# One value projection of 512 columns, a new place for the convolution, and another order of the first operations, in a two-block transformer kernel

## The chip, the core and the metric

The kernel runs as one program on one core of a Trainium2 chip. The time is device time in microseconds (us) of an execution, the median of several runs. Engines: PE is TensorE (its weight loads are listed as PEld), DVE is VectorE, ACT is ScalarE, POOL is GpSimd, SP is SyncE, whose queue issues all DMAs here. Each engine works through its own instructions in a fixed order; waits go over semaphores.

## What is computed

Two blocks of two layers each, on 512 tokens of width 1024, in f32. The change touches the first block. One layer of it, cut from the reference:

```python
x = x + 0.5 * swiglu(rmsnorm(x, ffn1_norm), ffn1_gate, ffn1_up, ffn1_down)
z = rmsnorm(x, mix_norm) @ w_in
(aq, ak, av, iq, ik, iw, bq, bk, bv, bg, br, cu, dcq, dckv, dkpe) = jnp.split(z, ...)
y_a = dsa_mixer(aq, ak, av, iq, ik, iw, ...)   # attention over 128 selected keys (top-k of an index score)
y_b = gla_mixer(bq, bk, bv, bg, br, ...)       # gated linear attention
y_c = conv_mixer(cu, ...)                      # depthwise convolution, 31 taps, 256 channels
y_d = mla_mixer(dcq, dckv, dkpe, ...)          # attention over latents
x = x + jnp.concatenate([y_a, y_b, y_c, y_d], axis=-1) @ w_out
x = x + 0.5 * swiglu(rmsnorm(x, ffn2_norm), ffn2_gate, ffn2_up, ffn2_down)
```

The second block has other mixers and the same kind of FFN; nothing of it is edited, though it uses the old `values`.

## The kernel before

The activations lie transposed, eight tiles `x[k]` of 128 channels by 512 tokens. A product in f32 is made of three in a rounded format (fp32r): a tile is split into a high part h and a residual l, and `mm3` adds h.h, h.l and l.h (lines 205, 206, 207 of `mm3`; PE instructions of these lines are told apart by the tile that they write). Weights come in one fixed list (`plan`, made of each stage's `order`). `fill` takes the next one from the list: a DMA of 128 x 1024 f32 (512 KB) into one of three `raw` buffers (line 188), the high part `wh` on ACT (line 190), the residual `wl` on DVE (line 191), each in one of four buffers (NW2). `weights(src)` keeps three of them filled and hands out the first.

A planner arranges the instructions of each engine before the run: of those that it takes to be ready at a moment it issues the one that stands first in the program; what is ready it reckons from modelled durations, DMAs included. The order on each engine is fixed after that, so an instruction that was put early and whose data comes late holds up all behind it on its engine.

**The beginning.** `begin` issues the first weight load, the x tiles and the second weight load, then for each k the head `xn[k]` h on ACT (`norm_head`, line 296), the residual on DVE (`norm_rest`, line 300), and the squares: ACT makes the square (`norm_square`, line 310, two buffers `sq`), POOL adds it to `sqacc` (line 311). PE later takes the mean `ms` (line 318) from `sqacc`. `dense_first` makes the first two weights' products: for each k both outputs' products with xn[k] h (lines 224 and 225), then those with the residuals (line 262). Outputs are scaled by the reciprocal root only when they are read from PSUM, so the products do not need `ms`. FFN outputs have six PSUM buffers.

**The mixers of the first block** (`Mixers.run`). In order: `a_keys`, `d_latents`, `a_queries`, `a_index`, `d_heads` (with four `uv` projections of 256 columns, line 1073 evicts them), `c_prep` (the projections `cu2`, `cu0`, `cu3`, `cu1`; the gated channels go to DRAM as `hp_d`). Then the D attention runs in eight steps, each with one round of the top-k on DVE and three steps of a side chain: `c_conv`, `a_values`, `a_heads` (projections aq0, aq1, ak0, ak1), `c_out`. After it: `b_heads` (bq, bk), `b_values`, `b_gates` (br0, br1), `a_bias` (loads `toep`), and then the A attention with the B mixer as its side chain.

`c_conv` loads each half of the channels from `hp_d` in shifted copies into the one buffer `gq` (four DMAs, line 995), then runs 32 matmuls on it (line 1000, each listed as two instructions); it yields after the loads and after the matmuls of each half, so conv1's load can start only when conv0's matmuls have read the buffer. `values` (line 590 on) has the activations as the stationary operand and two weights of 4 x 256 columns as the moving one: four token tiles x 8 k x 3 products of 256 columns, called once for A (`av`) and once for B (`bv`).

Of the kernel before, what the change touches and what calls it, by code (L numbers as in the profile page):

```python
# [9 lines left out]
F32 = mybir.dt.float32  # L10
# [10 lines left out]
KD = D // 128  # L21
# [11 lines left out]
def pack_values(w):  # L33

    return np.ascontiguousarray(w.reshape(2, 4, 128, 256).transpose(0, 2, 1, 3))

# [25 lines left out]
class Model:  # L62
# [115 lines left out]

    def fill(self, n):
# [62 lines left out]
    def dense_first(self, srcs, name, parts):  # L242
# [50 lines left out]
    def norm_head(self, k, gain, c=slice(0, S)):  # L293
        if c.start == 0:
            self.xn[k] = self.xn_tile(f"xn{k}h"), self.xn_tile(f"xn{k}l")
        self.nc.scalar.activation(self.xn[k][0][:, c], self.x[k][:, c], AF.Copy, scale=self.vec(gain, 1, k))

    def norm_rest(self, k, gain, c=slice(0, S)):
        h, l = self.xn[k]
        self.nc.vector.scalar_tensor_tensor(l[:, c], self.x[k][:, c], self.vec(gain, 1, k), h[:, c].bitcast(F32),  # L300
                                            op0=ALU.mult, op1=ALU.subtract)

    def norm_square(self, k, eng=None):
        nc = self.nc
        if self.sq_acc is None:
            self.sq_acc = self.tmp.tile([128, S], F32, name="sqacc", tag="sqacc", bufs=1)
            nc.scalar.activation(self.sq_acc, self.x[k], AF.Square)
            return
        sq = self.sq()
        nc.scalar.activation(sq, self.x[k], AF.Square)  # L310
        (eng or nc.gpsimd).tensor_tensor(self.sq_acc, self.sq_acc, sq, op=ALU.add)  # L311
# [71 lines left out]
NRAW = 3  # L383
NW2 = 4
# [98 lines left out]
def host_pack_mixers(I, P, vadd):  # L483
    for l in range(2):
# [9 lines left out]
        P[f"w_v{l}"] = np.stack([pack_values(w[:, IN_OFF[n]:IN_OFF[n] + 256]) for n in ("av", "bv")])  # L494
# [109 lines left out]


# [65 lines left out]
class Mixers(Phase):  # L671


    def order(self):
# [3 lines left out]
        v = lambda i: [ap[f"w_v{l}"][i, c] for c in range(2)]  # L678
        return p("misc", "dcq0", "dcq1", "dckv", "iq0", "iq1") + [ap[f"d_uq{l}"], ap[f"d_ukv{l}"]] + \
            p("cu2", "cu0", "cu3", "cu1") + v(0) + p("aq0", "aq1", "ak0", "ak1", "bq", "bk") + v(1) + p("br0", "br1") + \  # L680
# [137 lines left out]
    def b_values(self):  # L818
        two = [self.z(f"vB{i}", f"R{i}") for i in range(2)]
        self.vB = [two[t // 2][:, 256 * (t % 2):256 * (t % 2) + 256] for t in range(4)]  # L820
        self.values(self.ap[f"w_v{self.l}"][1], lambda t: self.vB[t])

    def a_values(self):
        two = [self.z(f"vA{i}", f"R{2 + i}") for i in range(2)]
        self.vA = [two[t // 2][:, 256 * (t % 2):256 * (t % 2) + 256] for t in range(4)]
        self.values(self.ap[f"w_v{self.l}"][0], lambda t: self.vA[t])
# [213 lines left out]
    def d_heads(self):  # L1040
# [25 lines left out]
        for t in range(4):  # L1066
            o = M.psum_mm("uv")[:, :256]
            r = slice(t * 128, (t + 1) * 128)
            M.mm3(o, (ch[:, r], cl[:, r]), (ukv[0][:, 256:512], ukv[1][:, 256:512]), True, True)
            if t % 2 == 0:  # L1070
# [915 lines left out]
```

## Time and profile before

| | us |
|---|---|
| median of 3 runs | 3255.04 (3254.06 to 3256.03) |
| the profiled execution | 3250.12 |
| its span, first to last instruction | 3248.3 |
| PE busy | 3179.6 |
| DVE busy | 1719.9 |
| ACT busy | 1314.0 |
| POOL busy | 151.6 |

Matmuls are pipelined, and a matmul's listed duration holds the time that it takes to pass through the array; so the distance from one start to the next tells what a matmul costs in a row of them. The granted TensorE clock of the whole execution is 0.997 of full speed; in the first microseconds the clock column says 1.00 also where the distances are those of half speed.

### The profile page before, as it was taken

The numbers are of one execution on the slowest core, as the hardware profiler recorded it, in microseconds if no ns is written. First come the engines' busy times: TensorE is split into PE (matmuls) and PEld (weight loads), VectorE is DVE, ScalarE is ACT, GpSimd is POOL, SyncE is SP. The second block draws the span as 40 slices with busy tenths as digits, with TensorE's granted clock in tenths as the row PEclk, the third lists the DMA queues.
The fourth block names the chain that finished last, engine by engine and source line by source line (L and its number), as shares of the span: only waits on it lengthen the run. The fifth ranks groups of instructions, "written<-read, shape, count | busy, mean of one in ns | idle before, by whom it ended". The sixth has DMA issues, their size and how long they took to land.

```text
span 3248.3 us, 39097 instructions
## 1 busy us (share of the span) xinstructions
PE 3179.6 (98%) x15294; PEld 2560.3 (79%) x15298; DVE 1719.9 (53%) x2788; ACT 1314.0 (40%) x2040; POOL 151.6 (5%) x153
## 2 busy tenths in 40 slices
PE   8999999999999999999999999999999999999998
PEld 6888866778888888875768888877888888788887
DVE  5443378664433444347775443588654427764432
ACT  4232345743322333244664332345643226753322
POOL 1000100010001000010000000100100010000000
PEclk9999999999999999999999999999999999999999
DMA  4333341133333333352113333322233332323332
GB/s 158 120 93 95 113 133 54 33 106 96 98 96 99 98 97 94 95 140 93 56 40 107 98 95 96 112 86 63 91 105 97 94 101 72 104 90 98 93 94 73
DMA packets 114473, 306.66 MB, mean 94 GB/s; under 512 B 21840, under 2 KB 35056, under 8 KB 114288
## 3 DMA queue, kind: packets, MB, share of 16 engines
q1 hardware_dynamic: 114288, 304.16, 31.2%
q8 instruction: 120, 1.97, 0.3%
q14 instruction: 65, 0.53, 0.0%
HBM read 292.18 MB, written 10.09 MB: 93 GB/s over the span
## 4 chain that ended last, share of the span: by engine, by line
PE 88%; ACT 4%; DVE 4%; DMA 2%; issue 1%; SPq 0%; POOL 0%; DVEq 0%; ACTq 0%
PE gu L206 14%; PE gu L205 14%; PE gu L207 14%; PE o L206 8%; PE o L205 8%; PE o L207 8%; DMA conv<-hp_d 2%; PE conv L1000 1%; PE wo L206 1%; PE wo L205 1%; PE wo L207 1%; PE v L207 1%; PE v L206 1%; PE v L205 1%; ACT gAqb L886 0%
## 5 line engine op out<-in xcount | busy, mean ns | idle before, releaser
L190 ACT ACTIVATE wh<-raw 128x1024 fp32r<-128x1024 f32 (+2 forms) x550 | 550.2, 1002 | 1479.3 <-PE gu L206 823.7
L191 DVE TENSOR_TENSOR wl<-raw,wh 128x1024 fp32r<-128x1024 f32 (+2 forms) x550 | 631.6, 1150 | 519.4 <-ACT wh L190 516.6
L205 PE MATMUL o<-hid,wh 128*128 128x512 f32 (+1 forms) x1100 | 419.2, 381 | 0.0
L206 PE MATMUL o<-hid,wh 128*128 128x512 f32 (+1 forms) x1100 | 418.9, 381 | 0.0
L207 PE MATMUL o<-hid,wl 128*128 128x512 f32 (+1 forms) x1100 | 418.5, 380 | 0.0
L351 DVE SCALAR_TENSOR_TENSOR us<-gu,rstd 128x512 f32<-128x512 f32 x130 | 89.9, 691 | 402.1 <-PE gu L207 401.7
L207 PEld LDWEIGHTS o<-hid,wl 128*128 128x128 f32 x1100 | 206.8, 188 | 39.8
L205 PEld LDWEIGHTS o<-hid,wh 128*128 128x128 f32 x1100 | 206.8, 188 | 39.6
L206 PEld LDWEIGHTS o<-hid,wh 128*128 128x128 f32 x1100 | 206.8, 188 | 39.3
L349 DVE SCALAR_TENSOR_TENSOR gs<-gu,rstd 128x512 f32<-128x512 f32 x130 | 89.9, 692 | 256.0 <-PE gu L207 255.3
L311 POOL TENSOR_TENSOR sqacc<-sqacc,sq 128x512 f32<-128x512 f32 x49 | 82.8, 1690 | 1580.6 <-ACT sq L310 1540.6
L354 ACT ACTIVATE hid<-gs 128x512 fp32r<-128x512 f32 x132 | 83.7, 634 | 94.8 <-DVE gs L352 94.8
L205 PE MATMUL gu<-xn0h,wh 128*128 128x512 f32 x254 | 101.3, 399 | 0.0
L206 PE MATMUL gu<-xn6l,wh 128*128 128x512 f32 x254 | 99.0, 390 | 1.9 <-DVE xn6l L300 1.9
L352 DVE TENSOR_TENSOR gs<-gs,us 128x512 f32<-128x512 f32 x132 | 91.3, 692 | 15.7 <-ACT gs L350 3.8
L206 PE MATMUL gu<-xn0l,wh 128*128 128x512 f32 x254 | 98.9, 389 | 0.0
L207 PE MATMUL gu<-xn1h,wl 128*128 128x512 f32 x254 | 98.9, 389 | 0.0
L205 PE MATMUL gu<-xn1h,wh 128*128 128x512 f32 x254 | 98.8, 389 | 0.0
L207 PE MATMUL gu<-xn0h,wl 128*128 128x512 f32 x254 | 98.8, 389 | 0.0
L206 PE MATMUL gu<-xn1l,wh 128*128 128x512 f32 x254 | 98.8, 389 | 0.0
L206 PE MATMUL gu<-xn2l,wh 128*128 128x512 f32 x254 | 98.8, 389 | 0.0
L205 PE MATMUL gu<-xn7h,wh 128*128 128x512 f32 x254 | 98.8, 389 | 0.0
(1438 smaller groups left out, 7079.1 us busy)
## 6 DMA issues: line engine op xcount, KB each, us to landing
raw<-in_ffn_gu SPq DMA_DIRECT2D x176, 512.0 KB
raw<-in_f_gu SPq DMA_DIRECT2D x88, 512.0 KB
raw<-in_ffn_d SPq DMA_DIRECT2D x64, 448.0 KB
raw<-in_w_in SPq DMA_DIRECT2D x36, 512.0 KB
raw<-in_ffn_d SPq DMA_DIRECT2D x32, 512.0 KB
raw<-in_f_d SPq DMA_DIRECT2D x32, 448.0 KB
raw<-in_w_out SPq DMA_DIRECT2D x32, 256.0 KB
raw<-in_f_d SPq DMA_DIRECT2D x16, 512.0 KB
```

The source lines that it names most:

```text
L190: nc.scalar.activation(h, raw, AF.Copy)
L191: nc.vector.tensor_tensor(l, raw, h.bitcast(F32), op=ALU.subtract)
L205: t.matmul(out, lhsT=wh, rhs=xh, start=first, stop=False)
L206: t.matmul(out, lhsT=wh, rhs=xl, start=False, stop=False)
L207: t.matmul(out, lhsT=wl, rhs=xh, start=False, stop=last)
L311: (eng or nc.gpsimd).tensor_tensor(self.sq_acc, self.sq_acc, sq, op=ALU.add)
L349: nc.vector.scalar_tensor_tensor(gs, g, -1.0, self.nrstd, op0=ALU.mult, op1=ALU.mult)
L351: nc.vector.scalar_tensor_tensor(us, u, -1.0, self.nrstd, op0=ALU.mult, op1=ALU.mult)
L352: nc.vector.tensor_tensor(gs, gs, us, op=ALU.mult)
L354: nc.scalar.activation(h, gs, AF.Copy)
L1000: nc.tensor.matmul(p[32 * g:32 * g + 32], lhsT=cw[:, g, k], rhs=st[:, g, 4 * k:4 * k + S], start=(k == 0), stop=(k == 7))
```

## The change

- `pack_wide` and `values_wide`: the A and B value weights are packed side by side, as four weights of 2 x 512 columns. One call, `ab_values`, makes both: four token tiles x 8 k x 3 products of 512 columns, one eviction per token tile, and it yields after each token tile. All four weights are held until the last token tile.
- The list of weights has the four value weights ahead of aq0; `b_values` after the D attention is gone.
- The side chain becomes: conv0's loads, the values, conv0's matmuls, conv1's loads, `a_heads`, conv1's matmuls, `c_out`.
- `d_heads`: the four `uv` projections go by twos into one PSUM tile, with one eviction of 512 columns each.
- `begin`: x tiles and halves (512 columns) of the first two weights are loaded in turn; the halves are split by ACT and DVE as they come. The order of ACT (heads and half copies, then squares) and of DVE (half residuals, xn residuals, then the additions of the squares, which leave POOL) is fixed by added dependencies without waits. 12 products of the constant `ones` tile with itself (128 x 128) go to a PSUM tile that nothing reads.
- `dense_first` for this beginning takes the first four k of the first output, then of the second, then the other four k of both.

```diff
+    def fill_part(self, i, part):
+        nc = self.nc
+        if part == 0:
+            src = self.todo.popleft()
...
+        c = slice(part * 512, part * 512 + 512)
+        nc.sync.dma_start(raw[:, c], flat[:, c])
+        if part == 1:
+            self.loaded.append((src, (h, l)))
+        return (lambda: nc.scalar.activation(h[:, c], raw[:, c], AF.Copy),
+                lambda: nc.vector.tensor_tensor(l[:, c], raw[:, c], h[:, c].bitcast(F32), op=ALU.subtract))
...
         for c in parts:
-            if c.start or not n:
+            if len(parts) == 1:
+                for o, w in zip(outs, ws):
+                    self.heads_first([o], [w], c, range(0, 4))
+                self.heads_first(outs, ws, c, range(4, KD))
+            elif c.start or not n:
                 self.heads_first(outs, ws, c)
...
+    def values_wide(self, w, out):
+        M, nc = self.M, self.nc
+        ws = [M.weights(w[c]) for c in range(4)]
+        for t in range(4):
+            r = slice(t * 128, (t + 1) * 128)
+            o = M.psum_mm("v")
+            for k in range(KD):
+                s = slice((k % 2) * 512, (k % 2) * 512 + 512)
+                M.mm3(o, (M.xn[k][0][:, r], M.xn[k][1][:, r]), (ws[k // 2][0][:, s], ws[k // 2][1][:, s]), k == 0, k == KD - 1)
+            nc.scalar.activation(out(t), o, AF.Copy, scale=self.rn[:, t:t + 1])
+            yield
...
-            p("cu2", "cu0", "cu3", "cu1") + v(0) + p("aq0", "aq1", "ak0", "ak1", "bq", "bk") + v(1) + p("br0", "br1") + \
+            p("cu2", "cu0", "cu3", "cu1") + v + p("aq0", "aq1", "ak0", "ak1", "bq", "bk", "br0", "br1") + \
...
-        for t in range(4):
-            o = M.psum_mm("uv")[:, :256]
...
+        for i in range(2):
+            o = M.psum_mm("uv")
+            dv = self.z(f"dv{i}", f"dv{i}")
+            for t in range(2):
...
+            nc.scalar.activation(dv, o, AF.Copy)
...
-            side = chain(self.c_conv, self.a_values, self.a_heads, self.c_out)
+            conv = self.c_conv()
+            part = lambda: next(conv)
+            side = chain(part, self.ab_values, part, part, self.a_heads, part, self.c_out)
...
-            self.b_values()
...
         def begin():
             M.norm_begin()
+            M.halved, split = [], []
             for k in range(KD):
-                if k in (0, 2):
-                    M.fill(1 + k // 2)
                 M.load_x(k)
+                if k < 4:
+                    split.append(M.fill_part(k // 2, k % 2))
+            head = lambda k: M.norm_head(k, "ffn1_norm0")
+            act, vec = [], []
             for k in range(KD):
-                M.norm_head(k, "ffn1_norm0")
-                M.norm_rest(k, "ffn1_norm0")
-            for k in range(KD):
-                M.norm_square(k)
+                act.append(head(k))
+                if k < 4:
+                    h, l = split[k]
+                    act.append(h())
+                    vec.append(l())
+            vec += [M.norm_rest(k, "ffn1_norm0") for k in range(KD)]
+            both = [M.norm_square(k, nc.vector) for k in range(KD)]
+            M.in_order(act + [a for a, _ in both])
+            M.in_order(vec + [v for _, v in both[1:]])
+            warm = M.psum("warm")
+            for i in range(WARM):
+                nc.tensor.matmul(warm[:, :128], lhsT=M.sumsq_ones, rhs=M.sumsq_ones, start=True, stop=True)
```

`in_order(ops)` adds such a dependency from each operation of the list to the next; `WARM` is 12.

## Rows read from the trace of the kernel before

**Rows 1.** The page, busy time and share of the span of each engine
```profile
PE 3179.6 (98%) x15294; PEld 2560.3 (79%) x15298; DVE 1719.9 (53%) x2788; ACT 1314.0 (40%) x2040; POOL 151.6 (5%) x153
```
**Rows 2.** The page, chain of work that ended last, share by engine
```profile
PE 88%; ACT 4%; DVE 4%; DMA 2%; issue 1%; SPq 0%; POOL 0%; DVEq 0%; ACTq 0%
```
**Rows 3.** PE's waits: in total, times, the longest
```profile
PE conv L1000 <- DMA conv<-hp_d: 12.5, 8, 2.8
...
PE uv L205 <- ACT uk L1060: 0.7, 2, 0.3
```
**Rows 4.** PE in order of time, beginning: start, duration, operation [idle before <-releaser]
```profile
7.19 0.80 PE L224 MATMUL gu<-xn0h,wh 128*128 128x512 f32 x1 [7.19 <-ACT xn0h L296]
...
11.73 0.63 PE L224 MATMUL gu<-xn1h,wh 128*128 128x512 f32 x1
...
14.66 0.39 PE L225 MATMUL gu<-xn3h,wl 128*128 128x512 f32 x1
...
22.51 1.13 PE L318 MATMUL ms<-sqacc,ones 128*128 128x512 f32 x2 [2.24 <-POOL sqacc L311]
...
28.05 0.39 PE L205 MATMUL gu<-xn0h,wh 128*128 128x512 f32 x1
...
33.27 0.39 PE L207 MATMUL gu<-xn7h,wl 128*128 128x512 f32 x1
```
**Rows 5.** ACT in order of time, beginning
```profile
20.00 0.71 ACT L296 ACTIVATE xn7h<-x,vecs 128x512 fp32r<-128x512 f32 x1
```
**Rows 6.** POOL in order of time, beginning
```profile
10.83 11.62 POOL L311 TENSOR_TENSOR sqacc<-sqacc,sq 128x512 f32<-128x512 f32 x7 [9.64 <-ACT sq L310]
```
**Rows 7.** Stretches: us, busy of PE, PEld, DVE, ACT, POOL, PEclk, DMA share, GB/s
```profile
0.00:5.00 5.00, 0.00 (x0) 0.00 (x0) 0.17 (x2) 1.28 (x1) 0.66 (x9) 1.00 0.59 176
5.00:10.00 5.00, 1.77 (x3) 0.86 (x3) 2.24 (x3) 3.63 (x5) 0.00 (x0) 1.00 1.03 378
```
**Rows 8.** DVE in order of time, an operation of two inputs and 512 columns
```profile
576.56 0.69 DVE L191 TENSOR_TENSOR wl<-raw,wh 128x512 fp32r<-128x512 f32 x1 [2.51 <-ACT wh L190]
```
**Rows 9.** PE in order of time, a 128x128 f32 product and its follower
```profile
479.89 0.38 PE L1118 MATMUL lgD<-dk,dq 128*128 128x128 f32 x2
480.11 0.22 PE L1119 MATMUL lgD<-causal_bf,ident_bf 128*128 128x128 bf16 x1
```
**Rows 10.** PE in order of time, first and last of 23 value products in a row
```profile
477.13 0.28 PE L205 MATMUL v<-wh,xn0h 128*128 128x256 f32 x1
...
479.77 0.29 PE L206 MATMUL v<-wl,xn7h 128*128 128x256 f32 x1
```
**Rows 11.** The chain in order of time, 440 to 580 us: start, us, what
```profile
450.03 13.32 DMA conv<-hp_d
```
**Rows 12.** PE in order of time, conv's matmuls in layer 0 and (last) layer 1
```profile
460.67 1.05 PE L1000 MATMUL conv<-conv 128*32 128x512 f32 x2 [0.27 <-DMA conv<-hp_d]
463.39 3.63 PE L1000 MATMUL conv<-conv 128*32 128x512 f32 x28 [1.67 <-DMA conv<-hp_d]
...
484.60 1.04 PE L1000 MATMUL conv<-conv 128*32 128x512 f32 x2 [1.09 <-DMA conv<-hp_d]
488.36 1.30 PE L1000 MATMUL conv<-conv 128*32 128x512 f32 x2 [2.72 <-DMA conv<-hp_d]
...
491.17 1.66 PE L1000 MATMUL conv<-conv 128*32 128x512 f32 x2
...
1516.86 1.92 PE L1000 MATMUL conv<-conv 128*32 128x512 f32 x2 [2.80 <-DMA conv<-hp_d]
```
**Rows 13.** PE in order of time, first product of B's values and of br
```profile
562.25 0.36 PE L205 MATMUL v<-wh,xn0h 128*128 128x256 f32 x1
...
577.13 0.40 PE L205 MATMUL br<-xn0h,wh 128*128 128x512 f32 x1
```
**Rows 14.** ACT and DVE in order of time, a weight's two parts after the cu projections
```profile
459.23 1.06 ACT L190 ACTIVATE wh<-raw 128x1024 fp32r<-128x1024 f32 x1 [0.91 <-PE cu L206]
...
468.15 1.22 DVE L191 TENSOR_TENSOR wl<-raw,wh 128x1024 fp32r<-128x1024 f32 x1
```

More of the change, by code (lines that the diff above doesn't have):

```diff
@@ L35, in pack_values, with pack_wide @@
     return np.ascontiguousarray(w.reshape(2, 4, 128, 256).transpose(0, 2, 1, 3))
+def pack_wide(w):
+    return np.ascontiguousarray(w.reshape(4, 2, 128, 512).transpose(0, 2, 1, 3))
 def cols(v):
@@ L177, in plan, with in_order @@
         self.todo, self.loaded = deque(srcs), deque()
+    def in_order(self, ops):
+        for a, b in zip(ops, ops[1:]):
+            self.tc.add_manual_dep(b.ins, a.ins.name, mybir.DependencyInfo(
+                mybir.DependencyClass.NoSync, mybir.DependencyReason.DATA), reason="issue order")
+    def fill_part(self, i, part):
+        nc = self.nc
+        if part == 0:
+            src = self.todo.popleft()
+            flat = src.rearrange("p a b -> p (a b)")
+            raw = self.wp.tile([128, flat.shape[1]], F32, name="raw", tag="raw", bufs=NRAW)
+            h, l = (self.wp.tile([128, flat.shape[1]], FR, name=n, tag=n, bufs=NW2) for n in ("wh", "wl"))
+            self.halved.append((src, flat, raw, h, l))
+        src, flat, raw, h, l = self.halved[i]
+        c = slice(part * 512, part * 512 + 512)
[4 more added lines that the diff above has]
+                lambda: nc.vector.tensor_tensor(l[:, c], raw[:, c], h[:, c].bitcast(F32), op=ALU.subtract))
     def fill(self, n):
@@ L295, in norm_head @@
             self.xn[k] = self.xn_tile(f"xn{k}h"), self.xn_tile(f"xn{k}l")
-        self.nc.scalar.activation(self.xn[k][0][:, c], self.x[k][:, c], AF.Copy, scale=self.vec(gain, 1, k))
+        return self.nc.scalar.activation(self.xn[k][0][:, c], self.x[k][:, c], AF.Copy, scale=self.vec(gain, 1, k))
     def norm_rest(self, k, gain, c=slice(0, S)):
         h, l = self.xn[k]
-        self.nc.vector.scalar_tensor_tensor(l[:, c], self.x[k][:, c], self.vec(gain, 1, k), h[:, c].bitcast(F32),
+        return self.nc.vector.scalar_tensor_tensor(l[:, c], self.x[k][:, c], self.vec(gain, 1, k), h[:, c].bitcast(F32),
                                             op0=ALU.mult, op1=ALU.subtract)
@@ L383 @@
 NRAW = 3
+WARM = 12
 NW2 = 4
@@ L493, in host_pack_mixers @@
         P[f"w_in{l}"] = pack_T(np.concatenate(t, axis=1))
-        P[f"w_v{l}"] = np.stack([pack_values(w[:, IN_OFF[n]:IN_OFF[n] + 256]) for n in ("av", "bv")])
+        P[f"w_v{l}"] = pack_wide(np.concatenate([w[:, IN_OFF[n]:IN_OFF[n] + 256] for n in ("av", "bv")], axis=1))
         uq = I["d_uq"][l].reshape(256, 4, 96)
@@ L815, in a_attend, with ab_values @@
                 yield
[L818 to L826, printed above, removed]
+    def ab_values(self):
+        v = [self.z(f"vAB{t}", f"R{t}") for t in range(4)]
+        self.vA = [t[:, :256] for t in v]
+        self.vB = [t[:, 256:] for t in v]
+        yield from self.values_wide(self.ap[f"w_v{self.l}"], lambda t: v[t])
     def b_heads(self):
```

20 lines of the change are left out of this document (8 added, 12 removed).

## The prediction

> **What bounds the kernel now.** I read the busy times first: TensorE (PE) is busy for 98% of the span, and no other engine comes near it [rows 1]. The chain that ended last says the same: 88% of it is PE work, and the next engine holds 4% [rows 2]. So a microsecond is worth something only where PE waits, where it runs at its lower clock level, or where it does work that can be had cheaper. The second thing to look at is therefore what PE waits for. The longest total is the conv matmuls of the first block's two mixers, which wait for their own DMAs; the small `uv` projections wait a little for ScalarE [rows 3]. Two places follow from that: the beginning, and the stretch from about 459 us (and the same 1028 us later in layer 1, 1516.86 against 488.36 us [rows 12]) in which conv, values and the D attention share PE.
>
> In the beginning the first matmul starts at 7.19 us, and the third FFN weight's products (L205) only at 28.05 us [rows 4]. The 48 products of the first two weights lie between. At the later spacing of 0.227 us (23 steps from 28.05 to 33.27 us) they would need 10.9 us. Two things stretch them. First, from 11.73 to 14.66 us the products stand 0.42 us apart (7 steps) and last 0.63 us, then 0.39 us: 512 columns in 0.42 us is the 1.2 GHz level, 0.227 us the 2.4 GHz level. The rise came after PE had worked without a gap since about 9.7 us. Second, the last activation tile's head, xn7h, is written by ScalarE only at 20.00 us [rows 5], since ScalarE makes the squares in the same order and each waits for a buffer that GpSimd frees: seven additions in 11.62 us [rows 6]. The mean of squares `ms` sits in PE's order ahead of xn7h and waits 2.24 us for the same additions [rows 4].
>
> The DMAs are not the limit there: 0.88 MB had come by 5 us (176 GB/s) and 1.89 MB more by 10 us [rows 7]. The eight x tiles, two weights and the vectors are 3.2 MB; at the latter rate, 378 GB/s, they are in by about 11.2 us.
>
> **The change, part by part.**
>
> *Beginning.* Added: two more DMA issues on SP (four half loads of 256 KB in place of two of 512 KB), each copied by ScalarE and subtracted by VectorE as 512 columns; removed: GpSimd's seven additions, which go to VectorE at 0.69 us each for two-input 512-column work [rows 8] against 1.66. ScalarE's order becomes heads and half copies, then squares; VectorE's becomes four half residuals, eight xn residuals, then additions. So xn7h no longer follows the squares: it follows its DMA. With about 1 us for landing and copy I put it at 12.3 us (estimate from rows 7), against 20.00. After it PE still owes 4 head products and 16 products on xn..l, 20 x 0.227 = 4.5 us, so 16.9 us at the least. The residuals are 12 x 0.69 = 8.3 us on VectorE, which starts at about 6 us and waits for halves on the way, so xnl7 comes at 14.5 to 16.3 us. PE also has a queue: o1's first products need the third and fourth half load, so some 24 head products remain at about 9 us, 5.5 us at the upper level; then 16 more, 3.6 us: 18 us. I take 18.5 us for the end of the first two weights, 17 if nothing queues, and 20 if the clock falls back in the sparse first microseconds. Against 28.05 that is 8 to 11 us.
>
> What is late next is the third weight: its residual is one VectorE operation which may stand behind the seven additions, 4.8 us after 16.3, so 21.1, and 1.2 us itself: 22.3. Then PE waits from 18.5 to 22 and the gain is 6. I take **-8 us**, ends -5 and -11. `ms` and the reciprocal root cannot cost more: six PSUM buffers let PE run 4 weights of 24 x 0.227 = 5.4 us ahead.
>
> The 12 constant products need only `ones`, written at 1 us. A 128x128 f32 product is listed as two instructions and the next one starts 0.22 us later [rows 9], at the upper level; 0.44 at the lower: 12 x 0.44 = 5.3 us, from 1.1 to 6.4 us. PE is otherwise idle until 7.19, so they cost at most a microsecond of the first products, which wait for later tiles anyway. What they may give, 15 products at 0.23 instead of 0.42 (2.9 us), is inside the 18.5; if the clock does not rise, the end is 20.
>
> *Values as 512 columns.* 192 products of 256 columns per layer become 96 of 512. The former stand 0.120 us apart (22 steps, 477.13 to 479.77 us) [rows 10], the latter 0.227 [rows 4]: 96 x (0.240 - 0.227) = 1.2 us, **-2.4 us** for two layers. The Trainium skill, "TensorE: Matmul & The Clock Gate", section "Back-to-back issue gap", speaks against this edit: it gives a spacing of columns by clock plus a fixed 2.5 ns, so two 256s would cost only 2.5 ns more than one 512, by that estimate 0.5 us in two layers and a sum smaller by 1.9 us. The trace disagrees with 12 ns a pair.
>
> *uv.* Four PSUM tiles and evictions become two. PE waits 0.7 us for them in two layers [rows 3]; the products are the same. I take **-0.7 us**, ends 0 and -0.7.
>
> *Values of B moved, conv order.* In the kernel before, conv's matmuls come in PE's order straight after the `cu` projection, because they precede the values in the program; their DMAs are not there. One conv load takes 13.32 us from issue to landing [rows 11]. So PE does two instructions from 460.67 to 463.39 us where a run of 28 takes 3.63 (0.13 each): 2.5 us lost. For conv1 it waits 1.09 and 2.72 us, and from 483.51 to 491.17 us it does two pairs and six value products (1.2 us): 6.5 us lost. Layer 1 shows the same wait, 2.80 us [rows 12]. That makes 9 us per layer. VectorE and ScalarE, which the D attention needs, stand still meanwhile, so neither is a bound that would take the gain over.
>
> After the change conv0's DMAs are issued, then all values come, then conv0's matmuls, conv1's DMAs, the A projections, conv1's matmuls. From 459 us PE has 96 x 0.227 = 21.8 us of value products to do, and only the last quarter of each tile needs the fourth weight; six of eight k, 18 products, are 4.1 us: to 463.1, as the conv data lands. I count the 2.5 us as won. conv1's load then runs beside three more value tiles (16.3 us) and the A projections; I count 4.5 of 6.5 us, since the order is still fixed at compile time without knowing the DMA's real length. B's values leave the stretch from 562.25 to 577.13 us, where PE works on them and then on `br` before the A attention can start [rows 13]; they fill the holes instead, which is how holes become time. Their two weights are no longer queued on SP behind the toep loads.
>
> New wait: four value weights fill all four wh/wl buffers. The fourth is copied after `cu` at 459.23 us, as another weight is now, and its residual can be late on VectorE; it was 468.15 us for the weight after the two values [rows 14], but there VectorE stood behind `sp`, which stood behind conv. I take 1 us. The next weight, aq0, can be copied only when the last value tile has passed the first weight, 18 products or 4.1 us before its own start; copy and residual take 1.06 + 1.22 us [rows 14], so it fits unless VectorE is inside a top-k round; 1 us. What is queued behind those two on ScalarE and VectorE are the D attention's exponentials and the top-k. Ends: 0 and 6 us per layer. **Net -2.5 - 4.5 + 2 = -5 per layer, -10 us**, ends -18 and +3 (nothing won but 1.5 us per layer of new wait).
>
> Sum: -8 - 2.4 - 0.7 - 10 = **-21 us**. The profiled execution took 3250.1 us for a span of 3248.3; it would take 3229. The median of the runs, 3255.0, is 4.9 us above that execution, so the predicted median is **3234 us**.
>
> **The rivals.** (1) *The conv wait stays*: the planner again puts conv where PE looks free, ahead of its data. [rows 3, 12] speak for it: eight waits, in both layers alike. Then 3255 - 8 - 2.4 - 0.7 + 0 = 3244. (2) *Slower: the value weights starve the next ones.* While four weights hold all wh/wl buffers none is prepared; if aq0's residual stands behind one whole step of the D attention (eight steps from 479.89 [rows 9] to at most 577.13 us [rows 13]: 12 us), PE stops for 12 us, and again for layer 1, while conv's waits stay: 3255 - 11 + 24 = 3268. It decides from a net loss of 5.5 us per layer on. Against it: the copy can start 4.1 us early, and `wl` operations in that stretch are placed between top-k rounds. (3) *The beginning gives little*: `wl` of the third weight and `ms` stand behind the additions and PE waits to 25: -3, mixers as forecast: 3239. (4) *The holes close wholly* (both conv loads hidden, no new wait): 3255 - 10 - 2.4 - 0.7 - 18 = 3224, and a little less where conv also runs in one piece.
>
> **How the numbers follow.** Forecast with (4), which is its lower side: 0.66; (1) 0.15; (3) 0.09; (2) 0.08; nothing to see 0.02. The time is the forecast's, 3234. Range: low -21 and the ends of its terms (-11 - 2.4 - 0.7 - 18 = -32, and 4 more for conv in one piece): 3219; high -5 - 2.4 + 0 + 0 = 3248, which takes in (1) and (3). A measurement of this kernel tells about 0.2%, 6.5 us, from no change. Faster by more: 0.66 + 0.09 + 0.10 of (1) = 0.85; within: 0.05 of (1) + 0.02 + 0.01 = 0.08; slower: 0.07.
>
> **What would show each step.** Right: xn7h by 13 us, L205 of the third weight between 17 and 22 us, products 0.23 us apart from about 7 us on; value products 0.227 us apart, 96 per layer; conv's wait for its DMA from 12.5 to below 5 us; `br` and the A attention 7 us earlier relative to the start of the mixer. Wrong: a new long wait of the third weight or of `aq` for wl, conv's matmuls again in pairs with gaps, or a D attention that ends later than before relative to the mixer's start.

## The result, and the profile after

| | us |
|---|---|
| before, median of the runs beside it | 3254.55 (3251.99 to 3256.03) |
| after, median of 4 runs | 3222.69 (3222.01 to 3224.93) |
| ratio, 95% interval | 0.991 (0.9898 to 0.9923) |
| profiled execution, before and after | 3250.12 and 3222.01 |
| its span, before and after | 3248.3 and 3220.2 |

The change takes about 32 us off the median and 28.1 off the span of the profiled execution. The page of after, busy time by engine and the shares of the chain that ended last, answers to [rows 1, 2]:

```profile
PE 3171.1 (98%) x15126; PEld 2551.9 (79%) x15130; DVE 1723.1 (54%) x2797; ACT 1306.3 (41%) x2026; POOL 138.6 (4%) x146
...
PE 91%; ACT 4%; DVE 4%; issue 1%; DMA 0%; SPq 0%; DVEq 0%; ACTq 0%
```

The 2% that DMA held in the chain are gone. Of the saving in the spans, 8.5 us are PE busy time and the rest is time in which PE had stood idle. In PE's waits of after (total, times, the longest) the line of conv and that of `uv` [rows 3] no longer stand. The longest, and one that is new, are

```profile
PE lev L934 <- ACT gAqb L928: 4.3, 8, 1.2
...
PE bd L898 <- DVE bpd L895: 2.9, 2, 1.4
```

The first total was there before (4.4 us); the second was not, and it marks where part of the gain is given back: `bd`, a small product of the B mixer, waits for DVE.

**The beginning of after.** PE in order of time (start, duration, operation, [idle before <-releaser]) answers to [rows 4]; the products with xn[k] h in `dense_first` are now lines 252 and 253, `mm3` is lines 233 to 235:

```profile
1.05 5.49 PE L1988 MATMUL warm<-ones 128*128 128x128 f32 x24 [1.05 <-DVE eps L86]
6.62 0.57 PE L252 MATMUL gu<-xn0h,wh 128*128 128x512 f32 x1
...
10.16 0.50 PE L252 MATMUL gu<-xn3h,wh 128*128 128x512 f32 x1 [0.78 <-ACT xn3h L328]
10.50 0.40 PE L253 MATMUL gu<-xn3h,wl 128*128 128x512 f32 x1
...
19.59 0.39 PE L233 MATMUL gu<-xn0h,wh 128*128 128x512 f32 x1
...
27.75 1.02 PE L349 MATMUL ms<-sqacc,ones 128*128 128x512 f32 x2
```

From 10.50 us on nothing is missing: 40 products of 0.227 us lead to the third weight at 19.59 us (28.05 before), and `ms` waits for nothing. ACT and then DVE in the same stretch:

```profile
12.71 0.72 ACT L328 ACTIVATE xn7h<-x,vecs 128x512 fp32r<-128x512 f32 x1
```
```profile
15.94 0.74 DVE L332 SCALAR_TENSOR_TENSOR xn7l<-x,vecs,xn7h 128x512 fp32r<-128x512 f32 x1
16.60 0.69 DVE L342 TENSOR_TENSOR sqacc<-sqacc,sq 128x512 f32<-128x512 f32 x1
17.20 1.22 DVE L219 TENSOR_TENSOR wl<-raw,wh 128x1024 fp32r<-128x1024 f32 x1
18.34 0.68 DVE L342 TENSOR_TENSOR sqacc<-sqacc,sq 128x512 f32<-128x512 f32 x1
```

The third weight's residual stands between two additions and not behind seven, so PE does not wait for it.

**The mixer of layer 0 in after**, PE in order of time, answers to [rows 10, 12, 13]:

```profile
450.88 0.39 PE L233 MATMUL v<-wh,xn0h 128*128 128x512 f32 x1
...
456.10 0.39 PE L235 MATMUL v<-wh,xn7l 128*128 128x512 f32 x1
...
465.05 2.76 PE L1042 MATMUL conv<-conv 128*32 128x512 f32 x18
...
554.44 0.40 PE L233 MATMUL br<-xn0h,wh 128*128 128x512 f32 x1
...
566.33 1.08 PE L879 MATMUL pre<-misc,bup 128*128 128x512 f32 x2
```

Value products stand 0.227 us apart (23 steps), conv waits for no DMA, and `br` starts 22.7 us earlier than in [rows 13]. But `pre`, the small product with which the B mixer's gates begin, now comes after `br`; before it came 17 us ahead of it:

```profile
559.94 1.02 PE L837 MATMUL pre<-misc,bup 128*128 128x512 f32 x2
```

The conv waits of before had a second price. The stretch around them in before (us, busy of PE, PEld, DVE, ACT, POOL, PEclk, DMA share, GB/s):

```profile
482.00:495.00 13.00, 9.20 (x41) 4.29 (x39) 5.19 (x21) 3.88 (x16) 0.00 (x0) 0.87 0.38 117
```

Behind conv's wait of 2.72 us the granted clock fell to the 1.2 GHz level for part of the stretch (0.13 x 13 = 1.7 us of clock): the value products from 489.97 to 490.82 us stand 0.21 us apart instead of 0.12. Layer 1 shows the same (0.86 from 1512 to 1524 us). In after PE is busy without a gap from 450 to 490 us, and the clock reads 1.00.

**Where the time went.** For one mixer I added, tile by tile, the distances from each PE row to the next start, so that a wait is charged to the tile before it. The rows are to be read to 0.2 us. Layer 0, from the mixer's first projection to the next FFN, in us (the kernels other than before and after are the experiments below; "A/B stage" is `wo`, `lgA` and `gB`):

| kernel | mixer | conv | values | uv | A/B stage | the rest |
|---|---|---|---|---|---|---|
| before | 306.35 | 25.26 | 26.57 | 2.40 | 77.77 | 174.35 |
| after | 295.97 | 16.26 | 23.34 | 1.67 | 81.43 | 173.27 |
| order_narrow | 293.22 | 15.28 | 24.00 | 2.39 | 78.10 | 173.45 |
| wide_old_order | 309.63 | 25.50 | 24.96 | 2.40 | 82.82 | 173.95 |
| narrow_moved | 297.22 | 15.24 | 23.84 | 2.40 | 81.42 | 174.32 |
| begin_order_narrow | 296.13 | 18.00 | 25.36 | 1.67 | 77.63 | 173.47 |
| early_prep | 292.49 | 16.25 | 23.32 | 1.67 | 78.06 | 173.19 |
| gates_late | 299.77 | 16.28 | 23.31 | 1.66 | 79.27 | 179.25 |

After against before: conv -9.0, values -3.2, uv -0.7, the rest -1.1, A/B stage +3.7, together -10.4. Layer 1 gives -11.4 in the same way (conv -10.1). With -7.6 at the beginning that is -29.4 at the end of the first block; 1.3 us are given back in the second block. About 0.8 of it goes behind a wait that both kernels have there, 2.57 us of PE for ACT (tile `glu`): in the stretch around it the clock is lower in after, and not in before. After, then before:

```profile
2218.00:2226.00 8.00, 5.33 (x33) 4.04 (x32) 6.74 (x14) 5.49 (x12) 0.00 (x0) 0.79 0.50 158
```
```profile
2247.40:2255.40 8.00, 5.21 (x36) 3.13 (x34) 7.13 (x16) 6.12 (x14) 0.00 (x0) 1.00 0.52 160
```

The rest goes around 2742 us, where PE waits 1.4 us for a weight's residual (tile `xb`) instead of 0.5.

The medians lie 3.8 us further apart than the spans. The profiled execution of before, 3250.12, lies below all four runs of its median, and one reason shows. In its beginning the clock stays at 1.00 behind the 2.24 us wait of `ms` (20 to 30 us), while order_narrow, narrow_moved and only_mix, which begin in the same way, read 0.83 there and wide_old_order 0.66; their mixers start at 382.1 to 383.2 us, that of before at 380.45. Against those four the new beginning is worth 9 to 10 us at that point, and 7.6 against the execution of before that was profiled.

### The profile page after: what moved, and what is told of

The parts are those of the page before. It is cut to its first block, busy times and chain, and to the rows that moved or that the text cites. A ratio compares the mean times of both kernels' runs of the same rounds, so it can differ in the third digit from the quotient of the medians.

```text
span 3220.2 us, 38750 instructions
## 1 busy us (share of the span) xinstructions
PE 3171.1 (98%) x15126; PEld 2551.9 (79%) x15130; DVE 1723.1 (54%) x2797; ACT 1306.3 (41%) x2026; POOL 138.6 (4%) x146
## 4 chain that ended last, share of the span: by engine, by line
PE 91%; ACT 4%; DVE 4%; issue 1%; DMA 0%; SPq 0%; DVEq 0%; ACTq 0%
PE gu L233 14%; PE gu L234 14%; PE gu L235 14%; PE o L234 8%; PE o L235 8%; PE o L233 8%; PE conv L1042 1%; ACT gAqb L928 1%; PE v L233 1%; PE v L234 1%; PE v L235 1%; PE wo L233 1%; PE wo L234 1%; PE wo L235 1%; PE lgD L1160 1%
## 5 line engine op out<-in xcount | busy, mean ns | idle before, releaser
L218 ACT ACTIVATE wh<-raw 128x1024 fp32r<-128x1024 f32 (+3 forms) x548 | 547.9, 1002 | 1481.0 <-PE gu L234 815.8
L219 DVE TENSOR_TENSOR wl<-raw,wh 128x1024 fp32r<-128x1024 f32 (+3 forms) x548 | 629.4, 1150 | 497.0 <-ACT wh L218 491.3
L342 POOL TENSOR_TENSOR sqacc<-sqacc,sq 128x512 f32<-128x512 f32 x42 | 69.9, 1665 | 1544.3 <-ACT sq L341 1504.8
L233 PE MATMUL gu<-xn4h,wh 128*128 128x512 f32 x254 | 99.2, 391 | 0.0
L235 PE MATMUL gu<-xn6h,wl 128*128 128x512 f32 x254 | 98.8, 389 | 0.0
```

The source lines that it names most:

```text
L218: nc.scalar.activation(h, raw, AF.Copy)
L219: nc.vector.tensor_tensor(l, raw, h.bitcast(F32), op=ALU.subtract)
L233: t.matmul(out, lhsT=wh, rhs=xh, start=first, stop=False)
L235: t.matmul(out, lhsT=wl, rhs=xh, start=False, stop=last)
```

## The experiments

Each was compared with runs of before on the same chip (the medians of before there lie within 0.4 us of each other; beside after it was 3254.55):

| kernel | median, us | before, us | ratio, 95% interval |
|---|---|---|---|
| only_begin | 3244.32 | 3252.46 | 0.9974 (0.9964 to 0.9984) |
| only_mix | 3231.85 | 3252.46 | 0.9936 (0.9921 to 0.9950) |
| order_narrow | 3226.05 | 3252.46 | 0.9917 (0.9902 to 0.9932) |
| wide_old_order | 3258.51 | 3252.46 | 1.0019 (1.0010 to 1.0029) |
| early_prep | 3215.38 | 3252.81 | 0.9887 (0.9872 to 0.9901) |
| gates_late | 3226.79 | 3252.81 | 0.9920 (0.9906 to 0.9935) |
| begin_order_narrow | 3222.18 | 3252.81 | 0.9906 (0.9889 to 0.9922) |
| narrow_moved | 3235.06 | 3252.81 | 0.9945 (0.9930 to 0.9959) |
| no_warm | 3225.41 | 3252.40 | 0.9918 (0.9904 to 0.9932) |
| begin_order | 3224.42 | 3252.40 | 0.9914 (0.9900 to 0.9927) |
| pool_adds | 3230.51 | 3252.40 | 0.9934 (0.9920 to 0.9947) |
| prep_four_uv | 3216.08 | 3252.40 | 0.9889 (0.9876 to 0.9903) |

### The two halves of the change: only_begin and only_mix

only_begin is after with the mixers of before; only_mix is after with the beginning of before. In terms of the change, only_begin leaves out

```diff
-            self.b_values()
...
-            side = chain(self.c_conv, self.a_values, self.a_heads, self.c_out)
+            side = chain(part, self.ab_values, part, part, self.a_heads, part, self.c_out)
```

with the `uv` pairs and the list of weights that belong to it, and only_mix leaves out

```diff
-                if k in (0, 2):
-                    M.fill(1 + k // 2)
...
+            both = [M.norm_square(k, nc.vector) for k in range(KD)]
+            M.in_order(act + [a for a, _ in both])
+            M.in_order(vec + [v for _, v in both[1:]])
...
+                nc.tensor.matmul(warm[:, :128], lhsT=M.sumsq_ones, rhs=M.sumsq_ones, start=True, stop=True)
```

with the halved loads and the new order of `dense_first`.

> The beginning of the changed kernel alone; values, uv and conv order as before. Theory (the parts add, since PE bounds every stage between): 7 to 9 us less than before, all of it there when the third weight's products start (19.6 instead of 28.05 us), and unchanged to the end. Rival (a later stage takes it back, as the second block seems to take 1.2 us): less than 5 us.

> The mixers' part alone (512-column values, uv by twos, conv order); beginning as before. Theory (the parts add): 20 to 24 us less than before, conv's wait for its DMA gone, 10 to 11.5 us in each layer. Rival (the mixers gain only with the other beginning, by a different plan): below 15 us.

Measured: -8.1 and -20.6 us, both as expected, together -28.7 against the -28.1 of the spans (the medians' -31.9 lies 3 us further off). The parts add up as far as that spread allows. By the tiles that PE writes, its order in the mixers is that of before in only_begin and that of after in only_mix (but for two records of some 1500 that one trace of each pair lacks): the new beginning doesn't change it.

### The order alone, the wide form alone: order_narrow and wide_old_order

order_narrow is before with the new order of the side chain and nothing else:

```diff
-            side = chain(self.c_conv, self.a_values, self.a_heads, self.c_out)
+            conv = self.c_conv()
+            part = lambda: next(conv)
+            side = chain(part, self.a_values, part, part, self.a_heads, part, self.c_out)
```

wide_old_order is before with the wide values of A and B in the place of A's, and the old chain:

```diff
+            side = chain(self.c_conv, self.ab_values, self.a_heads, self.c_out)
...
-            self.b_values()
```

> Only the side chain's order is changed: conv0's loads, A's values in 256-column form, conv0's matmuls, conv1's loads, the A projections, conv1's matmuls; B's values stay after the D attention; beginning, uv and widths as before. Theory A (a closed hole is won time by itself): conv's wait for its DMA falls from 12.5 to below 3 us and 14 to 18 us are gained, 7 to 9 in each layer. Theory B (the stretch is bound by VectorE and ScalarE too, so that holes are worth something only when B's values move into them): waits gone, but 6 us gained at most.

> Only the 512-column values are changed, both made where A's were, behind both conv halves in the side chain; beginning, uv and conv's order as before. Theory A: conv still waits 10 us or more for its DMA, and only the cheaper products are won: 2 to 5 us. Theory B (B's values fill the holes wherever conv stands): 12 us or more, with conv's wait still there.

Measured: -26.4 us for the order alone, well beyond what I had given it, and +6.1 us for the wide form alone, which neither theory had. PE's waits in wide_old_order still hold

```profile
PE conv L1038 <- DMA conv<-hp_d: 11.6, 8, 2.7
```

while in order_narrow conv's matmuls come late and in long pieces (conv0 in PE's order of time):

```profile
467.00 1.05 PE L1041 MATMUL conv<-conv 128*32 128x512 f32 x2
...
469.26 2.78 PE L1041 MATMUL conv<-conv 128*32 128x512 f32 x24
...
473.73 1.06 PE L1041 MATMUL conv<-conv 128*32 128x512 f32 x8
...
475.15 3.63 PE L1041 MATMUL conv<-conv 128*32 128x512 f32 x30
```

So the order closes the hole, and more value products behind it don't: in the table conv costs 25.5 us with the wide values and 15.3 with the new order. The order makes the values cheaper as well (26.57 to 24.00 us), since conv no longer stands between them: 1.1 us of that is a conv wait [rows 12], which the table charges to the value product before it, and about 0.7 is the lower clock behind it. A short piece of conv costs as much as a longer one: from its start to the next PE row the piece of 2 takes 0.98 us, the piece of 8 takes 1.00, and in the piece of 24 an instruction costs 0.11. In wide_old_order the values' gain of 1.6 us is outweighed by 5.0 us more in the A/B stage; 1.4 of them are clock (0.83 from 598 to 608 us; in the same part of after it reads 1.00), the other 3.6 are as in after.

This also says what B's values did in the mixers. The order alone, with them in their old place, ran 5.8 us faster against before than the whole change of the mixers, only_mix (-26.4 and -20.6).

### Why the A/B stage takes longer: narrow_moved, early_prep, gates_late

What wide_old_order and after have in common is that B's values no longer stand between the D attention and `br`, and that `pre` comes after `br` (at 588.99 us in wide_old_order, `br` at 575.41). `pre` heads a chain over DVE and ACT (`la`, `gate_e`, the scan `bsum`, `lev_e`) that the B mixer's levels need.

narrow_moved is order_narrow with B's values, in 256 columns, moved into the side chain behind A's, and their weights moved up in the list:

```diff
-            side = chain(part, self.a_values, part, part, self.a_heads, part, self.c_out)
+            side = chain(part, self.a_values, self.b_values, part, part, self.a_heads, part, self.c_out)
...
-            self.b_values()
```

early_prep is after with the step that holds `pre` put ahead of `br` in the program:

```diff
             self.b_heads()
+            prep = self.b_prep()
+            next(prep)
             self.b_gates()
...
-            side = chain(self.b_prep, self.b_diag, self.b_levels, self.b_out)
+            side = chain(self.b_diag, self.b_levels, self.b_out)
```

gates_late is early_prep with `br` taken out of there and put into the side chain behind the levels:

```diff
-            self.b_gates()
-            side = chain(self.b_diag, self.b_levels, self.b_out)
+            side = chain(self.b_diag, self.b_levels, self.b_gates, self.b_out)
```

> As order_narrow, but B's values too stand in the side chain (256 columns, two weights held at a time), right behind A's. Theory M (it is B's early place that costs, by putting pre behind br): 18 to 22 us less than before, 5 or more us behind order_narrow, pre after br. Theory W (it is the four held weights that cost): 25 us or more less than before, as order_narrow.

> The changed kernel with B's gate preparation (its small matmul pre, the exponentials, the running sum) placed ahead of the br projections in the program, nothing else. Theory P (what the A and B stage gives back after br is the late start of the B chain, which waits for pre behind the br products): the running sum 10 to 14 us earlier relative to br's first product, 2 to 6 us less in each layer, 4 to 12 us less than the changed kernel. Theory Q (the stage is bound by the A attention's exponentials on ScalarE, whose start doesn't move): less than 2 us of difference.

> As the run before it, and the two br projections move behind B's seven levels in the side chain, so that they are filler for TensorE in the A and B stage. Theory P with free TensorE time in that stage: the A attention starts up to 11 us earlier in each layer and 6 to 16 us are won against the changed kernel. Theory Q, or that stage bound by TensorE: no more than early_prep, or slower than it by up to 5 us, since br's own splits come in the middle of the exponentials.

narrow_moved: -17.8 us, 9 us worse than order_narrow, and all of it is the move, the only edit between the two (in its profile 1.4 us of layer 1 are lower clock behind it). The A/B stage grows from 78.10 to 81.42 us, as in after, and PE shows `br` and then `pre`:

```profile
575.56 0.39 PE L235 MATMUL br<-xn7h,wl 128*128 128x512 f32 x1
...
576.77 1.08 PE L878 MATMUL pre<-misc,bup 128*128 128x512 f32 x2
```

The wide form is therefore not the cause; the early place of B's values is. In early_prep `pre` stands ahead of `br`, which follows at 554.10 us (PE):

```profile
553.64 1.02 PE L879 MATMUL pre<-misc,bup 128*128 128x512 f32 x2
```

DVE in before, in after and in early_prep:

```profile
572.24 1.23 DVE L846 TENSOR_TENSOR_SCAN bsum<-reset,la 128x512 f32<-128x512 f32 x1
...
590.00 0.41 DVE L878 TENSOR_TENSOR lev_e<-bsum 128x256 f32<-128x256 f32 x1
```
```profile
567.44 0.75 DVE L882 TENSOR_SCALAR la<-pre,vecs 128x512 f32<-128x512 f32 x1
...
575.13 1.20 DVE L888 TENSOR_TENSOR_SCAN bsum<-reset,la 128x512 f32<-128x512 f32 x1
...
578.15 0.41 DVE L920 TENSOR_TENSOR lev_e<-bsum 128x256 f32<-128x256 f32 x1
```
```profile
561.02 1.22 DVE L888 TENSOR_TENSOR_SCAN bsum<-reset,la 128x512 f32<-128x512 f32 x1
...
568.04 0.41 DVE L920 TENSOR_TENSOR lev_e<-bsum 128x256 f32<-128x256 f32 x1
```

In before the scan ran at 572.24 and `lev_e` only at 590.00 us: 17.8 us of slack, in which PE worked on B's values and `br`. In after `lev_e` follows the scan by 3.0 us, and PE goes short: `bd` waits 1.42 us for `bpd`, which DVE makes right behind the scan (at 576.25 us), and the A attention twice 0.7 us for DVE. The windows of 20 us after `br`, in after and then in early_prep (us, busy of PE, PEld, DVE, ACT, POOL, PEclk, DMA share, GB/s):

```profile
566.00:586.00 20.00, 17.12 (x95) 12.82 (x95) 11.92 (x35) 17.10 (x47) 0.52 (x1) 1.00 0.08 27
```
```profile
566.00:586.00 20.00, 19.58 (x115) 14.93 (x114) 13.96 (x45) 18.73 (x59) 0.00 (x0) 1.00 0.12 37
```

PE lacks 2.9 us in after and 0.4 in early_prep. early_prep ran 7.3 us faster than after (7.4 by the spans; 5.6 if each median is held against its own before), 37.4 us faster than before: faster than both kernels, and as expected.

gates_late was to show whether `br` is better spent where PE would otherwise wait. It lost 11.4 us against early_prep, more than the 5 us that had been allowed for. Its PE rows and windows:

```profile
560.47 0.40 PE L235 MATMUL br<-xn2h,wl 128*128 128x512 f32 x1
563.45 1.22 PE L852 MATMUL lgA<-ak,aq 128*128 128x256 f32 x2 [2.58 <-ACT PT L699]
...
564.99 0.78 PE L233 MATMUL br<-xn3h,wh 128*128 128x512 f32 x1
```
```profile
556.00:566.00 10.00, 6.84 (x34) 5.04 (x33) 6.01 (x18) 7.56 (x15) 0.58 (x1) 0.84 0.10 31
566.00:578.00 12.00, 12.00 (x49) 9.44 (x48) 3.96 (x10) 7.09 (x23) 0.00 (x0) 0.71 0.00 0
```

Without a solid block of `br` PE stands idle for 2.58 us at the start of the A attention, and the granted clock falls: 0.84 and 0.71 of full speed in the two windows, 0.16 x 10 + 0.29 x 12 = 5.1 us of clock, a little of it within the idle time. Both together are about the 7.3 us by which its mixer is longer than early_prep's. In early_prep the clock reads 1.00 in the same stretch. The block of `br` was worth its place as cover.

### The sum that didn't come: begin_order_narrow

It is after with the 256-column values, B's after the D attention: the beginning, the order and the `uv` pairs, without the move that costs.

```diff
-            side = chain(part, self.ab_values, part, part, self.a_heads, part, self.c_out)
+            side = chain(part, self.a_values, part, part, self.a_heads, part, self.c_out)
...
+            self.b_values()
```

> The changed kernel with the values back in 256-column form, A's in the side chain and B's after the D attention; new beginning, uv and conv order stay. Theory (the parts add): order_narrow's 26.4 us, the beginning's 8 and uv's 1.5: 36 us less than before, so 3 to 6 us less than the changed kernel. Rival (it was another plan that made order_narrow fast): 3223 us or more.

Measured: 3222.18 us, as after and not 6 us less. The table says where: conv costs 18.00 us and the values 25.36 us against 15.28 and 24.00 in order_narrow, 4.1 us more (3.4 in layer 1). The planner put conv earlier, and it waits again (PE's waits):

```profile
PE v L233 <- ACT vA L635: 2.3, 2, 1.2
...
PE conv L1045 <- DMA conv<-hp_d: 1.4, 2, 1.2
```

Two kernels whose side chains read the same came out with different orders on PE. They differ in the beginning and in the `uv` pairs, and the record points to the pairs. The new beginning alone left PE's order in the mixers as it was (only_begin as before, only_mix as after), while early_prep and prep_four_uv below, which differ in the pairs alone, part in PE's order, from the `cu` projections right behind `uv` on; there too order_narrow and begin_order_narrow part. A run of this kernel with four `uv` tiles would show it; there is none.

### The beginning: no_warm, begin_order, pool_adds

no_warm is after without the constant products:

```diff
-            warm = M.psum("warm")
-            for i in range(WARM):
-                nc.tensor.matmul(warm[:, :128], lhsT=M.sumsq_ones, rhs=M.sumsq_ones, start=True, stop=True)
```

begin_order has no constants either, and the old loads of two whole weights with the old order of `dense_first`; the fixed order and the additions on DVE stay:

```diff
+                if k in (0, 2):
+                    M.fill(1 + k // 2)
...
-                if k < 4:
-                    split.append(M.fill_part(k // 2, k % 2))
```

pool_adds is after with the additions back on POOL:

```diff
-            both = [M.norm_square(k, nc.vector) for k in range(KD)]
+            both = [M.norm_square(k) for k in range(KD)]
             M.in_order(act + [a for a, _ in both])
-            M.in_order(vec + [v for _, v in both[1:]])
+            M.in_order(vec)
```

> The changed kernel without the 12 constant products. Theory C (they bring the higher clock level forward): the first real products stand 0.43 us apart until 4 to 5 us after TensorE works without a gap, the third weight's products start 1.5 to 3.5 us later than at 19.59 us, and the time grows by as much. Rival (the last tile's head at 12.7 and the residuals up to 16.7 us set the end anyway): less than 0.5 us.

> The changed kernel's mixers with the beginning of the kernel before, in which only the order is fixed: heads ahead of the squares on ScalarE, residuals ahead of the additions on VectorE; whole 512 KB loads, no constant products. Theory O (the squares in front of the last head are the main cause): head of the last tile at 12 to 14 us, the third weight's products from 21 to 23.5 us, 2 to 4 us more than the changed kernel. Rival (half loads and clock carry it): 6 to 10 us more.

> The changed kernel with the additions of the squares back on GpSimd, everything else of the beginning as it is. Theory O (order is what counts, and the squares now come after the heads): within 1 us of the changed kernel. Rival (the additions' engine counts: ms comes later than the planner reckons and stops TensorE, as it did before the change): 2 to 5 us more, with a wait of ms for GpSimd.

PE's order in the mixers is that of after in all three, so what the beginning brings can be read at the first value product of layer 0: 450.88 us in after, 452.56 in no_warm, 452.05 in begin_order and 459.18 in pool_adds. In the six profiles with the whole new beginning the third weight starts between 18.91 and 19.96 us; a difference of half a microsecond says nothing here.

no_warm: 2.7 us slower than after by the medians, 1.7 of them in the beginning; in its profile another 1.4 stand in the A/B stage of layer 0, where the clock reads 0.83 (576 to 586 us) and which the edit doesn't touch. The first products stand 0.43 us apart, the 1.2 GHz level, up to 13.02 us, where after has 0.23 to 0.24 from the start wherever a product waits for nothing; PE in order of time:

```profile
12.59 0.63 PE L253 MATMUL gu<-xn1h,wl 128*128 128x512 f32 x1
13.02 0.51 PE L252 MATMUL gu<-xn2h,wh 128*128 128x512 f32 x1
...
21.35 0.39 PE L233 MATMUL gu<-xn0h,wh 128*128 128x512 f32 x1
```

The third weight comes 1.76 us later. Had every product of after come without a wait, the 12 slow ones would have cost 12 x 0.2 = 2.4 us; part of that falls into waits for tiles.

begin_order: 1.7 us slower than after, just less than the 2 to 4 expected, with xn7h at 12.09 us and the third weight at 20.81. So the fixed order with the additions on DVE is nearly the whole gain of the beginning, 6.4 of 7.6 us. It lacks the constants, the halved loads and the order of `dense_first`, and still comes no later than no_warm, which lacks the constants alone: without constants the other two show no gain. That the rest is the constants' is argued from these two runs; constants with whole loads were not run, nor the additions on DVE without the fixed order.

pool_adds: 7.8 us slower than after, as much as the whole beginning had brought and more than the rival's 2 to 5. PE, then DVE, then POOL:

```profile
22.31 0.40 PE L233 MATMUL gu<-xn2h,wh 128*128 128x512 f32 x1
27.39 2.07 PE L349 MATMUL ms<-sqacc,ones 128*128 128x512 f32 x2 [4.68 <-POOL sqacc L342]
28.47 1.42 PE L234 MATMUL gu<-xn2l,wh 128*128 128x512 f32 x1
29.69 0.63 PE L235 MATMUL gu<-xn2h,wl 128*128 128x512 f32 x1
```
```profile
14.83 0.74 DVE L332 SCALAR_TENSOR_TENSOR xn5l<-x,vecs,xn5h 128x512 fp32r<-128x512 f32 x1
15.49 1.78 DVE L332 SCALAR_TENSOR_TENSOR xn6l<-x,vecs,xn6h 128x512 fp32r<-128x512 f32 x1
17.20 1.77 DVE L332 SCALAR_TENSOR_TENSOR xn7l<-x,vecs,xn7h 128x512 fp32r<-128x512 f32 x1
18.89 4.54 DVE L219 TENSOR_TENSOR wl<-raw,wh 128x1024 fp32r<-128x1024 f32 x2
```
```profile
14.95 12.38 POOL L342 TENSOR_TENSOR sqacc<-sqacc,sq 128x512 f32<-128x512 f32 x7 [13.76 <-ACT sq L341]
```

The squares now come last, so seven additions of 1.77 us end at 27.3 us, and `ms` has a fixed place in PE's order: PE stops for 4.68 us, and the next products are at the 1.2 GHz level (0.43 us apart from 29.69 to 31.39 us). Besides, the DVE operations shown beside an addition take 1.04 us longer (0.74 becomes 1.78; 1.22 becomes 2.27), and PE waits 0.8 us for the third weight's residual.

### uv by fours: prep_four_uv

early_prep with four `uv` tiles and evictions of 256 columns:

```diff
-        for i in range(2):
-            o = M.psum_mm("uv")
+        for t in range(4):
+            o = M.psum_mm("uv")[:, :256]
```

> early_prep with the uv projections back in four tiles and four evictions. Theory U (uv by twos saves 0.7 us a layer and changes nothing else): 1 to 2 us more than early_prep. Rival (uv by twos shifts the plan of the conv stretch for the worse, as it seems to in the 256-column form, where the two layers together gained 5 us less with it): 2 to 5 us less than early_prep.

Measured: 3216.08 against 3215.38 us, 0.7 us slower, just less than the 1 to 2 expected: the sign of the 1.5 us in the table (0.73 in each layer), and half of it. Each of its two mixers is 1.1 us longer.

## Why the prediction was right, and where its steps were not

The time, 3222.69, lies in the range given, 11 us below the value named; the sign and the places were right. Four of the 11 us are no matter of the kernel: the prediction added 4.9 us from the profiled execution to the median, and in after that distance is 0.7. In the spans it forecast -21 and got -28.1. The closeness is in part luck, as the steps show:

- *Beginning, -8.* The spans show -7.6, and only_begin ran 8.1 us faster. xn7h came at 12.71 and was ready at 13.4 us, the third weight at 19.59: inside what was given. The rival of a third weight that waits to 25 us didn't occur, since the planner mixed the residuals with the additions. The constants, the halved loads and the order of `dense_first` brought about 1 us of it (begin_order lacks all three). One argument was wrong although nothing came of it here: that `ms` can't cost more because PSUM lets PE run ahead. PE's order is fixed, `ms` has its place in it, and pool_adds paid 4.68 us there.
- *Values, -2.4.* Too large. The spacing of 0.227 us came as forecast, but between narrow_moved and after, whose mixers differ in the form of the values and in the `uv` pairs, their cost falls from 23.84 to 23.34 us: 0.5 per layer. Products in an unbroken row would differ by 192 x 0.120 - 96 x 0.227 = 1.2 us, as forecast; but other matmuls stand between them, and the wide ones pay 1.5 us over the row for that, the narrow ones 0.8. The Trainium skill's estimate by "Back-to-back issue gap" ("TensorE: Matmul & The Clock Gate"), with the formula that the section gives for an isolated matmul, was 0.25 per layer; narrow products stand 0.120 us apart in order_narrow too, so that a pair takes 13 ns more than one wide product (not 12), which speaks against it. That the sum came out nearer to it lies in those other matmuls.
- *uv, -0.7.* Too small by half: 0.73 in each layer. I read the wait that was listed for PE and not the distances, in which the short gaps between the four tiles are counted too.
- *Holes, -7 per layer before the new waits.* This is the term that was mis-sized. I had counted 9 us of holes and taken 7 of them as won; conv's cost fell by 9.0 and 10.1 us, all of it, and the values' by another 2 to 2.6 us, since conv no longer stood between them. The lower clock behind the waits, 1.7 us per layer, is part of what the holes cost, and the prediction names it nowhere. Holes closed wholly is half of rival 4's condition; the other half, no new wait, failed. That the time lies near its 3224 is luck, all the more as its sum takes 10 us for the beginning where the forecast has 8. Rival 1 is what wide_old_order shows: with the old chain the wait stays (11.6 us). The reason given for part of the gain was wrong too: of B's values it says "they fill the holes instead, which is how holes become time", and order_narrow closed the holes with A's values alone.
- *New waits, +2 per layer.* The amount was short and the place wrong. `aq` took 0.1 us more, so the value weights starved nobody. What cost 3.7 us per layer was that B's values had been cover: PE work in whose shade `pre`, `la`, `gate_e` and the scan ran. I had asked who waits for what is added, and not what ran beside what is taken away. The prediction's line "`br` and the A attention 7 us earlier relative to the start of the mixer" shows it: `br` started 15.1 us earlier by that measure (22.7 - 7.6), and the mixer's end won only 10.4.

So the errors of the mixers' terms have opposite signs. For holes and values the sum had -8.2 us per layer and the traces show -12.2 and -12.9; for new waits it had +2 and they show +3.7 and +3.8. With `uv` and the rest of the mixer (-1.1 and -1.5) the net is -21.8 us for two layers where the sum had -13.

## What to carry to other kernels

When work stands in PE's order ahead of its data, more work behind it doesn't help (wide_old_order); put the load, then the other work, then its use into the program in that order. Before a block of PE work is moved, list what the other engines do beside it: the chain that ran in its shade has to move ahead too (here one step, worth about 7 us). Where a planner orders the engines, an edit in one place can move work in another: compare PE's order tile for tile before you add the gains of two edits. A squared-sum chain that feeds only a late scale factor still stops PE if its consumer has a fixed place in PE's order.

## What the runs showed of the hardware

- In pool_adds DVE operations beside POOL's additions took 1.04 us longer, at both sizes (0.74 to 1.78, 1.22 to 2.27 us), and the additions 1.77 us each; a cast of 128x128 with one input took 1.28 us instead of 0.22. In before the residuals xn2l to xn7l were lengthened by 0.17 to 1.00 us. The Trainium skill, "SBUF — State Buffer", section "Who interferes with whom", says that a VectorE instruction with two inputs in SBUF contends with a GpSimd instruction that reads SBUF. The trace agrees as far as the operations with two inputs go.
- A PE gap of 2.58 us in gates_late came with a granted clock of 0.84 and 0.71 over 10 and 12 us, one of 4.68 us in pool_adds with products at the 1.2 GHz level. So a gap can cost clock beside idle time, in gates_late about 5 us beside 2.58. Not every gap does: around the 2.57 us for which PE waits at `glu` the clock reads 0.79 over 8 us in after and 1.00 in before, and around the 2.2 us at `ms` 1.00 over 10 us in before and 0.83 in order_narrow. At such a place two profiles can differ by a microsecond or two without an edit.
